# One key tile between a head's scores and its exponential, GpSimd in program order, one slot for reciprocals and result, and filler matmuls moved to later attention units

## The chip, the cores and the metric

The kernel runs on one core of a Trainium2 chip. The time is device microseconds of one execution of the program. The time before is the median of three runs. One more execution was recorded by the hardware profiler; all rows shown here come from that one.

## The reference

An encoder layer is run over two requests that share their weights: a sample of 1024 tokens and a prompt of 256, each with 16 learned meta tokens in front (1040 and 272 positions, width 1024, float32 throughout). The part that matters here is the attention and what follows it at once:

```python
def attention_block(qb, k, v):
    scale = HEAD_DIM ** -0.5
    s = jnp.einsum('bqhgd,bshd->bhgqs', qb, k).astype(jnp.float32) * scale
    p = jax.nn.softmax(s, axis=-1).astype(v.dtype)
    return jnp.einsum('bhgqs,bshd->bqhgd', p, v)
...
    g_attn = jax.nn.sigmoid(z[..., o3:o4])
    g_four = jax.nn.sigmoid(z[..., o4:])
...
    a = bidirectional_gqa(q, k, v) @ w_attn_o
    fo = fourier_mix(f) @ w_four_o
    merged = g_attn * a + g_four * fo
    x = x + merged @ w_out
```

There are 8 query heads of width 64 in 2 groups; each group of 4 shares one key head and one value head. Before this stage come the norm, the input projections and a Fourier branch; after it the merge, the output projection and a SwiGLU network.

## The kernel before

**Precision.** Every product is made of float32 operands split into a high and a low part (`split`), three matmuls for one (`three`, lines 231 to 233).

**Attention.** `attention` goes over units: a query tile of 128 tokens and a key group, four heads each. The prompt's tiles 8 and 9 come first (4 units), then the sample's tiles 0 to 7 (16 units). For one head (lines 994 to 1024):

- PE computes the scores of all keys into a PSUM tile `S` (line 1001): two matmuls for the prompt's 272 keys, six for the sample's 1040. `S` has one buffer. A sample head takes it whole, so the next head's scores wait for this head's exponential; three prompt heads fit in it side by side.
- VectorE takes the negated maximum (line 1006).
- ScalarE takes the exponential into a slot `p`, with the row's sum behind it (line 1013); VectorE later replaces the sum by its reciprocal (line 1019).

**The second half of a unit** is an object `Second`. It has one turn for each key tile: 9 in a sample unit, 3 in a prompt unit. A turn transposes a key tile of the four heads' probabilities on PE (line 915, two PSUM buffers `pt`), copies the high part on ScalarE (line 926) and subtracts for the low part on VectorE (line 927). The product with the values (lines 948, 949, 953, PSUM `pv`) follows some turns later. The last turn takes the 16 meta keys and the column of reciprocals, whose transposed row VectorE copies to a slot `rc` (line 919); SP writes it to DRAM and reads it back broadcast over 64 partitions (line 956). The two halves of `pv` are copied to a slot `ao` by ScalarE and VectorE (957, 958), added and multiplied by the reciprocals on GpSimd (959, 960), and stored to `a_d` (964).

The turns of a unit begin one head after its last head. `turns(0)` runs them between the next unit's maximum and exponential, `turns(1)` behind the exponential. The count for each call spreads what is left evenly over eight half heads: a sample unit gets 2 in front and 1 behind in its first head, then 1 and 1 three times.

**Filler.** After each half, `attention` yields a kind, and `gates` (a `Filler` around `gate_gen`) runs matmuls of the gate projection (tile `g`) until the debt `FILL[kind]` is paid: 12 units of weights by 768 columns, 576 matmuls in all, in steps of three. A step of 512 columns counts 640, one of 256 columns 320. If no unit is waiting for its second half, 1000 is added. What is left runs after the last key tile, beside the loads of the merge.

**Order.** In this stage PE, ScalarE and VectorE run in program order (`manual_schedule`). GpSimd and SP get their order from the framework's scheduler. On GpSimd there are also the low parts of the filler's weights (line 585) and, from the 97th yield on, one step per head of `fourier_parts`: memsets, casts (line 1069) and subtractions for the Fourier tail.

**Slots.** All tiles in SBUF come from 27 single slots and 7 triples. A slot that is given back goes to the end of a queue; whoever gets it next waits until its last reader is done.

**After attention** `load_af` reads `a_d` back (line 1100) and splits it (215, 216); `merge` multiplies the Fourier part (tile `fo`) and then the attention part (tile `m`), the sample's second half of tokens last.

Of the kernel before, what the change touches and what calls it, by code (L numbers as in the profile page):

```python
# [12 lines left out]
ALU = mybir.AluOpType  # L13
# [4 lines left out]
P = 128  # L18
# [4 lines left out]
HD = 64  # L23
# [28 lines left out]
LEAD = (2, 2, 2, 2, 2, 3, 3)  # L52
FINISH = (1, 3, 5, 7, 9)
LAG = 6000
XLOAD = 3
DVELO = (1,)
THIRDS = ((512, 1024), (0, 256), (256, 512))
# [79 lines left out]
def f32(ap):  # L137
    return ap.bitcast(F32)
# [44 lines left out]
class Kernel:  # L183
# [377 lines left out]

    FILL = {"s": 420, "p": 500, "end": 480, "drain": 900}

    def gate_gen(self, chunks, lo_engine):

# [312 lines left out]
    def attention(self, ps, tiles, tag_s, tag_v):  # L880


        nc, sl = self.nc, self.sl
        units = [(t, g) for t in tiles for g in range(NKV)]
        q = self.q

        def load_q(i):
            if i < len(tiles):
                self.load_q(tiles[i])

        load_q(1)

        mt = sl.get("mt", F32R)
        nc.gpsimd.memset(f32(mt[:, :1024]), 0.0)

        class Second:


            def __init__(me, i, t, g, ps4, slots):
                me.i, me.t, me.g, me.ps4, me.slots = i, t, g, ps4, slots  # L900
                n = 8 if t < 8 else 2
                me.keys = [(self.V[i if t < 8 else 8 + i], P, i * P) for i in range(n)]
                me.keys.append((self.V[10], N_META, n * P))
                me.j, me.pv = 0, None

            def left(me):
                return len(me.keys) - me.j

            def turn(me):
                V, rows, col = me.keys[me.j]  # L910
                pt = ps.tile([P, 512], F32, tag="tr", name=f"pt{me.t}{me.g}{me.j}")
                last = me.left() == 1
                for h in range(4):
                    m = rows + last
                    nc.tensor.transpose(pt[:m, h * P : (h + 1) * P], me.ps4[h][:, col : col + m], self.ident[:])  # L915
                if last:

                    me.rc = sl.get("rc")
                    nc.vector.tensor_copy(me.rc[:m, 512:1024], pt[:m, :])
                    nc.sync.dma_start(self.rc_d[me.t][me.g : me.g + 1, :], me.rc[rows:m, 512:1024])  # L920
                    pT, b = None, me.i % 2 * 512
                    hi, lo = mt[:rows, b : b + 512], mt[32 : 32 + rows, b : b + 512]
                else:
                    pT = sl.get("pT", F32R)
                    hi, lo = pT[:, :512], pT[:, 512:1024]
                nc.scalar.copy(hi, pt[:rows, :])  # L926
                nc.vector.tensor_tensor(lo, pt[:rows, :], f32(hi), op=ALU.subtract)  # L927

                if len(late) >= 2 and not (late[0][1] == 0 and len(late) == 2):
                    product()  # L930
                    if len(late) == 2:
                        product()
                late.append((me, me.j, pT))
                me.j += 1
                if me.j == len(me.keys):
                    sl.put(*me.slots)

        late = deque()

        def product():  # L940
            me, j, pT = late.popleft()
            t, g = me.t, me.g
            if j == 0:
                me.pv = ps.tile([P, 512], F32, tag=tag_v, name=f"pv{t}{g}")
            V = me.keys[j][0]
            vst = V[:, g * P : (g + 1) * P]
            if pT is not None:
                nc.tensor.matmul(me.pv[:], vst, pT[:, :512], start=j == 0, stop=False)
                nc.tensor.matmul(me.pv[:], vst, pT[:, 512:1024], start=False, stop=False)
                sl.put(pT)  # L950
                return
            b = me.i % 2 * 512
            nc.tensor.matmul(me.pv[:], vst, mt[:, b : b + 512], start=False, stop=True)
            aos = sl.get("ao")

            nc.sync.dma_start(me.rc[:HD, :512], self.rc_d[t][g].partition_broadcast(HD))
            nc.scalar.copy(aos[:HD, :512], me.pv[HD:P, :])
            nc.vector.tensor_copy(aos[:HD, 512:1024], me.pv[:HD, :])
            nc.gpsimd.tensor_tensor(aos[:HD, :512], aos[:HD, :512], aos[:HD, 512:1024], op=ALU.add)
            nc.gpsimd.tensor_tensor(aos[:HD, :512], aos[:HD, :512], me.rc[:HD, :512], op=ALU.mult)  # L960
            sl.put(me.rc)
            off = (t % 4) * P if t < 8 else (t - 8) * P
            dst = self.a_d[t // 4][:].rearrange("(h d) n -> d h n", d=HD)
            nc.sync.dma_start(
                dst[:, 4 * g : 4 * g + 4, off : off + P], aos[:HD, :512].rearrange("d (h n) -> d h n", h=4)
            )
            sl.put(aos)

        queue, n, divide, S = deque(), 0, None, None

        def turns(k):

            for me, ready in list(queue):
                if n < ready:
                    return
                for _ in range(-(-me.left() // (2 * (ready + 4 - n) - k))):
                    me.turn()
                if me.left():
                    return
                queue.popleft()  # L980

        for i, (t, g) in enumerate(units):
            if g == 0:
                i0 = tiles.index(t)
                load_q(i0 + (2 if i0 < 3 else 1))
            if t < 8:
                seq, L, cuts = "s", LS, (0, 264, 776, LS)
            else:
                seq, L, cuts = "p", LP, (0, LP)

            per, wide = SLOT // (L + 1), L + 1
            ps4, slots = [], []
            for h in range(4):
                hq = q[t][:, (4 * g + h) * P : (4 * g + h + 1) * P]

                if S is None or t < 8:
                    S = ps.tile([P, 1536], F32, tag=tag_s, name=f"S{t}{g}{h}")
                base = 248 if t < 8 else (4 * i + h) % 3 * 512
                for lo, hi in zip(cuts, cuts[1:]):
                    for v in range(2):  # L1000
                        nc.tensor.matmul(  # L1001
                            S[:, base + lo : base + hi], hq, self.kT[seq][g][v][:, lo:hi], start=v == 0, stop=v == 1
                        )
                sm = self.small.tile([P, 4], F32, tag="sm", name="sm", bufs=4)
                nb = sm[:, 0:1]
                nc.vector.tensor_reduce(nb, S[:, base : base + L], axis=AX.X, op=ALU.max, negate=True)  # L1006
                turns(0)
                if divide:
                    divide()
                if h % per == 0:  # L1010
                    slots.append(sl.get("p"))
                p = slots[-1][:, (h % per) * wide : (h % per + 1) * wide]
                self.last_exp = nc.scalar.activation(  # L1013
                    p[:, :L], S[:, base : base + L], AF.Exp, bias=nb, accum_out=p[:, L:wide]
                )
                yield "end" if i + 1 == len(units) else seq, 0, False

                def divide(x=p[:, L:wide]):
                    nc.vector.reciprocal(x, x)

                ps4.append(p)
                turns(1)
                yield "end" if i + 1 == len(units) else seq, 0 if queue else 1000, True
                n += 1
            if g == NKV - 1:
                sl.put(q.pop(t))
                if t == 9:
                    sl.put(*self.kv_slots[4:6])
                if t == tiles[-1]:
                    sl.put(*self.kv_slots[:4])  # L1030
            queue.append((Second(i, t, g, ps4, slots), n + 1))
        divide()
        while queue:
            for half in range(2):
                turns(half)
                yield "drain", 0, True
            n += 1
        while late:
            product()
        sl.put(mt, *self.kv_slots[6:])  # L1040


# [231 lines left out]
    def w_out(self, tiles, ps, then=None, apart=False):  # L1274
# [37 lines left out]
        for half in range(2):  # L1312
# [15 lines left out]
            for kk in range(4):  # L1328
                i = half * 4 + kk
                need(i + 1)  # L1330
                if apart and kk >= 2:
                    need(i + 3)
                if i == XLOAD:
                    for t in tiles:
# [43 lines left out]
    def second_norm(self, u, v, chunk, off, gf, ps):  # L1378
# [3 lines left out]
        hs = [self.h2.pop(t) for t in (u, v)]  # L1382
        yield LAG

# [366 lines left out]
    def build(self):  # L1751
        sl = self.sl
# [23 lines left out]
        units = self.ffn_units()  # L1776
        w1 = self.w_out((4, 6, 5, 7), ps_e, units, True)
        w02 = self.w_out((0, 2, 1, 3, 8, 9), ps_e, w1)
        m = self.merge(w02)
        with self.psum("pd", {"S": (1, 1536), "tr": 2, "pv": 1, "g": 2}) as ps:  # L1780
            E = mybir.EngineType
            self.mm = ps, "g"
            with self.tc.manual_schedule(engines={E.PE, E.Activation, E.DVE}):
                later = self.later = deque()
                parts = self.fourier_parts()
                for i, (kind, more, slack) in enumerate(self.attention(ps, [8, 9] + list(range(8)), "S", "pv")):
# [179 lines left out]
```

## Time and profile before

| | us |
|---|---|
| median of three runs | 1725.2 (1723.81 to 1730.75) |
| the profiled execution | 1728.47 |
| its span, first to last instruction | 1726.7 |
| attention, first scores to the last exponential | 317 to 644 |
| PE busy in the span | 1648.2 (95%) |

Times in the rows are microseconds from the span's start unless a row says ns. In a row of the timeline stand start, duration, engine, line, operation, out<-in, shape and count, and in brackets the idle time of the engine before it with what ended it. In a group's row (line, engine, operation, shape, count) stand the busy time in us and the mean ns of one, then the idle time before them by releaser. A matmul's duration runs to its modelled end, while the next one starts earlier. Names like `hT0l` or `fx` in place of `pT` or `wgl` are slots that were part of a triple.

### The profile page before, as it was taken

How to read it: one execution, taken by the hardware profiler on the slowest of the kernel's cores; microseconds unless marked ns; L12 is line 12 of the kernel's file. 1: busy time of each engine (PE TensorE's matmuls, PEld its weight loads, DVE VectorE, ACT ScalarE, POOL GpSimd, SP SyncE). 2: the span in 40 equal slices, each digit the busy share in tenths (PEclk: the TensorE clock that was granted, in tenths of full speed). 3: DMA queues.
4: the chain of work that ended last, by engine and by line, in shares of the span. 5: the costliest groups of instructions: out<-in, count | busy, mean ns of one | idle time of the engine just before them, and what ended most of it. 6: DMA issues, size and time to landing. Idle time of an engine off the chain costs nothing.

```text
span 1726.7 us, 26025 instructions
## 1 busy us (share of the span) xinstructions
PE 1648.2 (95%) x9739; PEld 1474.7 (85%) x9739; DVE 1100.5 (64%) x2028; ACT 727.4 (42%) x1463; POOL 355.1 (21%) x400
## 2 busy tenths in 40 slices
PE   7999999989979998999989999999999999999998
PEld 6888879867767786878879999999999998888886
DVE  5563555346756766661489676667666768765685
ACT  6433333446656765551355222222232224444444
POOL 3451443232242323563352000000000000000002
PEclk9999999999999999999999999999999999999999
DMA  6135231421111226533432222322232237653534
GB/s 247 42 124 176 98 115 46 149 62 62 50 49 59 65 80 222 164 128 117 176 142 81 89 72 86 103 90 88 91 103 91 69 122 258 207 179 93 164 96 153
DMA packets 92454, 198.76 MB, mean 115 GB/s; under 512 B 10230, under 2 KB 41622, under 8 KB 92328
## 3 DMA queue, kind: packets, MB, share of 16 engines
q1 hardware_dynamic: 82296, 179.63, 31.4%
q10 hardware_dynamic: 8400, 12.53, 2.1%
q0 software_dynamic: 1632, 4.93, 0.9%
q8 instruction: 77, 1.26, 0.3%
q14 instruction: 49, 0.40, 0.1%
HBM read 141.58 MB, written 55.47 MB: 114 GB/s over the span
## 4 chain that ended last, share of the span: by engine, by line
PE 72%; DVE 9%; ACT 7%; issue 4%; POOL 4%; DMA 3%; SPq 0%; ACTq 0%; POOLq 0%; DVEq 0%
PE i L233 10%; PE i L231 10%; PE i L232 10%; PE o L233 5%; PE o L232 5%; PE o L231 5%; PE S L1001 4%; ACT p L1013 2%; PE pt L915 2%; PE g L231 2%; PE g L232 2%; PE g L233 2%; DVE sm L1006 2%; PE wo L232 2%; PE wo L233 2%
## 5 line engine op out<-in xcount | busy, mean ns | idle before, releaser
L1458 ACT CAST w<-wi 128x512 fp32r<-128x512 f32 x168 | 104.0, 621 | 272.1 <-PE i L233 219.0
L231 PE MATMUL i<-A,w 128*128 128x384 f32 x616 | 209.1, 339 | 3.0 <-ACT w L1458 2.7
L233 PE MATMUL i<-A,w 128*128 128x384 f32 x616 | 209.0, 340 | 2.3 <-POOL w L1460 2.3
L232 PE MATMUL i<-A,w 128*128 128x384 f32 x616 | 208.6, 339 | 0.0
L231 PE MATMUL i<-Ah,w 128*128 128x256 f32 x616 | 173.0, 281 | 0.7 <-DVE sc L1514 0.7
L232 PE MATMUL i<-Al,w 128*128 128x256 f32 x616 | 173.0, 281 | 0.0
L233 PE MATMUL i<-Ah,w 128*128 128x256 f32 x616 | 173.0, 281 | 0.0
L240 POOL TENSOR_SCALAR fin0r<-fin0ss 128x1 f32<-128x1 f32 x1 | 0.8, 785 | 755.7 <-ACT X L248 755.7
L1460 DVE TENSOR_TENSOR w<-wi,w 128x512 fp32r<-128x512 f32 x154 | 105.4, 686 | 28.8 <-ACT w L1458 28.3
L927 DVE TENSOR_TENSOR pT<-pt,pT 128x512 fp32r<-128x512 f32 x117 | 80.0, 686 | 65.5 <-ACT pT L926 65.0
L231 PEld LDWEIGHTS i<-A,w 128*128 128x128 f32 x616 | 116.7, 189 | 3.6 <-ACT w L1458 2.9
L233 PEld LDWEIGHTS i<-A,w 128*128 128x128 f32 x616 | 116.7, 189 | 3.0 <-POOL w L1460 2.9
L231 PEld LDWEIGHTS i<-Ah,w 128*128 128x128 f32 x616 | 116.1, 188 | 1.4 <-DVE sc L1514 0.9
L232 PEld LDWEIGHTS i<-A,w 128*128 128x128 f32 x616 | 116.7, 189 | 0.0
L233 PEld LDWEIGHTS i<-Ah,w 128*128 128x128 f32 x616 | 116.2, 189 | 0.0
L232 PEld LDWEIGHTS i<-Al,w 128*128 128x128 f32 x616 | 116.1, 189 | 0.0
L1006 DVE TENSOR_REDUCE sm<-S 128x1 f32<-128x1040 f32 (+1 forms) x80 | 86.4, 1081 | 36.8 <-PE S L1001 32.2
L926 ACT CAST pT<-pt 128x512 fp32r<-128x512 f32 x117 | 68.4, 585 | 76.6 <-PE pt L915 65.1
L915 PE MATMUL pt<-ident,p 128*128 128x128 f32 (+1 forms) x624 | 94.7, 275 | 3.4 <-DVE pT L927 2.7
L1013 ACT ACTIVATE p<-S,sm 128x1040 f32<-128x1040 f32 (+1 forms) x80 | 80.1, 1001 | 37.2 <-DVE sm L1006 28.5
L915 PEld LDWEIGHTS pt<-ident,p 128*128 128x128 f32 (+1 forms) x624 | 72.4, 135 | 16.3 <-DVE pT L927 6.0
L233 PE MATMUL o<-wfo,act 128*128 128x512 f32 (+1 forms) x212 | 82.0, 388 | 1.6 <-DVE act L1592 1.6
(812 smaller groups left out, 4529.9 us busy)
## 6 DMA issues: line engine op xcount, KB each, us to landing
wi<-w_fi SPq DMA_DIRECT2D x48, 512.0 KB
act_d<-sc SPq DMA_DIRECT2D x77, 192.0 KB
wg<-w_g SPq DMA_DIRECT2D x24, 512.0 KB
act<-act_d SPq DMA_DIRECT2D x37, 320.0 KB
wfo<-w_fo SPq DMA_DIRECT2D x21, 512.0 KB
X<-act_d SPq DMA_DIRECT2D x31, 320.0 KB
act_d<-sc SPq DMA_DIRECT2D x77, 128.0 KB
gt<-gate SPq DMA_DIRECT2D x32, 256.0 KB
```

Of the source, the lines that this page charges most:

```text
L231: mm(out, sh, mh, start=first and i == 0, stop=False)
L232: mm(out, sh, ml, start=False, stop=False)
L233: mm(out, slo, mh, start=False, stop=last and i == n - 1)
L240: nc.gpsimd.tensor_scalar(r[:p, 0, :n], ss, scale, eps, op0=ALU.mult, op1=ALU.add)
L915: nc.tensor.transpose(pt[:m, h * P : (h + 1) * P], me.ps4[h][:, col : col + m], self.ident[:])
L926: nc.scalar.copy(hi, pt[:rows, :])
L927: nc.vector.tensor_tensor(lo, pt[:rows, :], f32(hi), op=ALU.subtract)
L1001: nc.tensor.matmul(S[:, base + lo : base + hi], hq, self.kT[seq][g][v][:, lo:hi], start=v == 0, stop=v == 1)
L1006: nc.vector.tensor_reduce(nb, S[:, base : base + L], axis=AX.X, op=ALU.max, negate=True)
L1013: self.last_exp = nc.scalar.activation(p[:, :L], S[:, base : base + L], AF.Exp, bias=nb, accum_out=p[:, L:wide])
L1458: nc.scalar.copy(w[:, :512], src)
L1460: eng.tensor_tensor(w[:, 512:1024], src, f32(w[:, :512]), op=ALU.subtract)
```

## The change

1. `turns`: the count is now a goal for each head, a quarter of the key tiles per head, and at most one turn stands between maximum and exponential. A sample unit has (1 in front, 2 behind), then (1, 1) three times; a prompt unit has one in front in each of three heads.
2. The slot `rc` is gone: the row of reciprocals is copied into partitions 64 to 80 of `ao`, which is taken at the last turn instead of at the last product, and the broadcast goes into the half of `ao` that the addition has read. So it follows the addition.
3. The multiplication, the store and the giving back of `ao` are kept in `leaving` and issued at the third call of `leaves` after the product, two heads later; in the drain `leaves` is called after each half.
4. GpSimd is added to the engines that run in program order.
5. `FILL` has new values, the first sample unit has its own kind `first`, the addition without a waiting unit is 150 instead of 1000, and the drain's kind is `end` while two units wait.

```diff
+FIRST = 4
-    FILL = {"s": 420, "p": 500, "end": 480, "drain": 900}
+    FILL = {"s": 550, "p": 150, "first": 1150, "end": 550, "drain": 600}
...
-                    me.rc = sl.get("rc")
-                    nc.vector.tensor_copy(me.rc[:m, 512:1024], pt[:m, :])
-                    nc.sync.dma_start(self.rc_d[me.t][me.g : me.g + 1, :], me.rc[rows:m, 512:1024])
+                    ao = me.ao = sl.get("ao")
+                    nc.vector.tensor_copy(ao[64 : 64 + m, :512], pt[:m, :])
+                    nc.sync.dma_start(self.rc_d[me.t][me.g : me.g + 1, :], ao[64 + rows : 64 + m, :512])
...
-            aos = sl.get("ao")
-            nc.sync.dma_start(me.rc[:HD, :512], self.rc_d[t][g].partition_broadcast(HD))
-            nc.scalar.copy(aos[:HD, :512], me.pv[HD:P, :])
-            nc.vector.tensor_copy(aos[:HD, 512:1024], me.pv[:HD, :])
-            nc.gpsimd.tensor_tensor(aos[:HD, :512], aos[:HD, :512], aos[:HD, 512:1024], op=ALU.add)
-            nc.gpsimd.tensor_tensor(aos[:HD, :512], aos[:HD, :512], me.rc[:HD, :512], op=ALU.mult)
-            sl.put(me.rc)
...
+            ao = me.ao
+            nc.scalar.copy(ao[:HD, :512], me.pv[HD:P, :])
+            nc.vector.tensor_copy(ao[:HD, 512:1024], me.pv[:HD, :])
+            nc.gpsimd.tensor_tensor(ao[:HD, :512], ao[:HD, :512], ao[:HD, 512:1024], op=ALU.add)
+            nc.sync.dma_start(ao[:HD, 512:1024], self.rc_d[t][g].partition_broadcast(HD))
+            def leave():
+                nc.gpsimd.tensor_tensor(ao[:HD, :512], ao[:HD, :512], ao[:HD, 512:1024], op=ALU.mult)
...
+                sl.put(ao)
+            leaving.append([2, leave])
+        def leaves(all=False):
+            while leaving and (all or leaving[0][0] <= 0):
+                leaving.popleft()[1]()
+            for x in leaving:
+                x[0] -= 1
...
-                for _ in range(-(-me.left() // (2 * (ready + 4 - n) - k))):
+                goal = -(-len(me.keys) * min(n - ready + 1, 4) // 4)
+                if k == 0:
+                    goal = min(goal, me.j + 1)
+                while me.j < goal:
                     me.turn()
...
-                yield "end" if i + 1 == len(units) else seq, 0, False
+                kind = "end" if i + 1 == len(units) else "first" if t < 8 and i <= FIRST else seq
+                yield kind, 0, False
...
                 turns(1)
-                yield "end" if i + 1 == len(units) else seq, 0 if queue else 1000, True
+                leaves()
+                yield kind, 0 if queue else 150, True
...
                 turns(half)
-                yield "drain", 0, True
+                leaves()
+                yield "drain" if len(queue) < 2 else "end", 0, True
...
         while late:
             product()
+        leaves(True)
...
-            with self.tc.manual_schedule(engines={E.PE, E.Activation, E.DVE}):
+            with self.tc.manual_schedule(engines={E.PE, E.Activation, E.DVE, E.Pool}):
```

More of the change, by code (lines that the diff above doesn't have):

```diff
@@ L936, in turn @@
                     sl.put(*me.slots)
-        late = deque()
+        late, leaving = deque(), deque()
         def product():
@@ L953, in product @@
             nc.tensor.matmul(me.pv[:], vst, mt[:, b : b + 512], start=False, stop=True)
-            aos = sl.get("ao")
[L956 to L960, printed above, removed]
-            sl.put(me.rc)
[L962 to L967, printed above, removed]
+            ao = me.ao
[5 more added lines that the diff above has]
+                nc.gpsimd.tensor_tensor(ao[:HD, :512], ao[:HD, :512], ao[:HD, 512:1024], op=ALU.mult)
+                off = (t % 4) * P if t < 8 else (t - 8) * P
+                dst = self.a_d[t // 4][:].rearrange("(h d) n -> d h n", d=HD)
+                nc.sync.dma_start(
+                    dst[:, 4 * g : 4 * g + 4, off : off + P], ao[:HD, :512].rearrange("d (h n) -> d h n", h=4)
+                )
+                sl.put(ao)
[5 more added lines that the diff above has]
+                x[0] -= 1
         queue, n, divide, S = deque(), 0, None, None
```

## The prediction

> **What bounds the kernel now.** The page first, then stretches, waits and timeline.
>
> ```profile
> PE 1648.2 (95%) x9739; PEld 1474.7 (85%) x9739; DVE 1100.5 (64%) x2028; ACT 727.4 (42%) x1463; POOL 355.1 (21%) x400
> ```
>
> TensorE (PE) is busy for 95% of the span, an average that hides the stage in question: every instruction that the diff touches lies between 317 and 690 us. So I read the table of stretches there, cut where the program turns from prompt attention to the first sample unit, the other 15 sample units, the drain and the tail. Columns: length, busy time of PE, weight loads, VectorE (DVE), ScalarE (ACT), GpSimd (POOL), granted clock, DMA share, GB/s.
>
> ```profile
> 317.10:359.50 42.40, 40.66 (x240) 34.22 (x238) 17.28 (x45) 21.07 (x57) 12.80 (x10) 1.00 0.32 106
> 359.50:377.80 18.30, 14.17 (x78) 11.63 (x77) 8.55 (x13) 8.57 (x15) 5.11 (x4) 0.91 0.25 73
> 377.80:643.80 266.00, 243.06 (x1457) 202.78 (x1458) 181.36 (x281) 170.70 (x303) 73.69 (x62) 0.99 0.18 56
> 643.80:667.40 23.60, 20.64 (x132) 17.61 (x130) 12.07 (x20) 12.21 (x22) 2.58 (x2) 1.00 0.73 249
> 667.40:690.00 22.60, 17.77 (x91) 15.48 (x92) 15.72 (x24) 11.52 (x20) 11.77 (x16) 0.85 0.62 207
> ```
>
> The prompt stage is full; the other four leave PE idle for 4.1, 22.9, 3.0 and 4.8 us. The same stretches for the filler alone (tile g, the gate product) show why: the full stage has most of it.
>
> ```profile
> 317.10:359.50 42.40, 31.79 (x161) 1.00 0.32 106
> 359.50:377.80 18.30, 7.28 (x37) 0.91 0.25 73
> 377.80:643.80 266.00, 71.45 (x312) 0.99 0.18 56
> ```
>
> 161 of the filler's 576 matmuls run where attention needs PE for little, and the long sample stage, which waits, has 312 for 60 heads. Who waits there, from the table of waits (total, times, longest):
>
> ```profile
> PE S L1001 <- ACT p L1013: 20.0, 20, 7.2
> ACT pT L926 <- DMA a_d<-ao: 4.8, 5, 1.3
> ```
>
> Scores of the next head wait for the exponential of this one, because a sample head has the one S buffer. The timeline shows two shapes of it. The starts of five heads, and the copies in front of the third one's exponential:
>
> ```profile
> 519.93 0.28 PE L1001 MATMUL S<-hT0l,qT 128*128 128x264 f32 x1
> 523.68 1.22 PE L1001 MATMUL S<-kT,qT 128*128 128x264 f32 x6
> 527.60 1.12 PE L1001 MATMUL S<-kT,qT 128*128 128x264 f32 x6
> 530.10 0.59 ACT L926 CAST pT<-pt 128x512 fp32r<-128x512 f32 x1 [0.32 <-PE pt L915]
> 530.71 0.58 ACT L957 COPY p<-pv 64x512 f32<-64x512 f32 x1
> 531.32 1.13 ACT L1013 ACTIVATE p<-S,sm 128x1040 f32<-128x1040 f32 x1
> 532.59 1.22 PE L1001 MATMUL S<-kT,qT 128*128 128x264 f32 x6 [0.31 <-ACT p L1013]
> 536.63 1.10 PE L1001 MATMUL S<-kT,qT 128*128 128x264 f32 x6
> ```
>
> They start 3.75, 3.92, 4.99 and 4.04 us apart. The long one is the head with three key tiles: two come before the exponential, and the second one's copy plus the copy of the finished result (0.59 + 0.58) hold ScalarE. That is 1.1 us once in four heads. The other shape comes once:
>
> ```profile
> 508.22 3.21 POOL L1069 CAST hT0l<-x64r 8x1024 fp32r<-8x1024 f32 x3
> 511.51 1.25 POOL L960 TENSOR_TENSOR ao<-ao,rc 64x512 f32<-64x512 f32 x1
> 512.79 1.13 ACT L1013 ACTIVATE p<-S,sm 128x1040 f32<-128x1040 f32 x1 [6.63 <-POOL ao L960]
> 514.06 0.59 PE L1001 MATMUL S<-hT0l,qT 128*128 128x264 f32 x1 [7.20 <-ACT p L1013]
> ```
>
> Three casts that GpSimd was given ahead of the division kept the result's slot, the exponential wanted that slot, and PE stood 7.2 us. Its matmuls then run at half clock (0.59 for a shape that took 0.28), for a window:
>
> ```profile
> 514.80:518.30 3.50, 3.50 (x13) 3.00 (x12) 2.29 (x3) 1.51 (x3) 0.38 (x1) 0.53 0.36 97
> ```
>
> **The change part by part.** No matmul is added or removed, so the sum is over idle time.
>
> *Filler.* The debts, counted by the code's own costs (a step of three matmuls is 640 at 512 columns, 320 at 256; a filler unit is 7680, all twelve 92160): prompt stage 32 yields x 500 + 10 x 1000 = 26.0 us, now 32 x 150 + 7 x 150 = 5.85; first sample unit 8 x 420 + 2 x 1000 = 5.36, now 8 x 1150 + 150 = 9.35; the other 15 units 112 x 420 + 8 x 480 = 50.9, now 112 x 550 + 8 x 550 = 66.0; drain 9.0, now 550 + 9 x 600 = 5.95; the rest, run after the last key tile, 0.92, now 5.01. On the chip the unit is larger:
>
> ```profile
> 317.42 0.40 PE L231 MATMUL g<-hT1h,wgh 128*128 128x512 f32 x1
> 319.98 0.40 PE L233 MATMUL g<-hT1h,wgl 128*128 128x512 f32 x1
> ```
>
> First and last of twelve in a row: 2.56 / 11 = 0.233 us from start to start, so 0.70 for 640: factor 1.09.
>
> *Prompt stage.* PE loses 20.15 x 1.09 = 22.0 us of work. If PE stayed the bound, 40.66 - 22.0 = 18.7 us would be left. But then the other engines' turns show, from the groups of this stage:
>
> ```profile
> L1013 ACT ACTIVATE p<-S,sm 128x272 f32<-128x272 f32 x16 | 7.8, 487 | 11.5 <-DVE sm L1006 10.2 <-issue 1.3
> L1006 DVE TENSOR_REDUCE sm<-S 128x1 f32<-128x272 f32 x16 | 7.0, 439 | 17.7 <-PE S L1001 17.0 <-ACT wgh L584 0.5 <-issue 0.2
> L927 DVE TENSOR_TENSOR pT<-pt,pT 128x512 fp32r<-128x512 f32 x5 | 3.5, 692 | 4.7 <-ACT pT L926 4.7
> L926 ACT CAST mt<-pt 16x512 fp32r<-16x512 f32 x3 | 1.7, 578 | 4.7 <-DVE rc L919 4.7
> L958 DVE COPY ao<-pv 64x512 f32<-64x512 f32 x2 | 1.4, 683 | 0.0
> ```
>
> A head with a key tile costs VectorE 0.44 + 0.69 and a reciprocal, ScalarE 0.49 + 0.58 and a read of the sum, in turn: about 1.5 us with the hand-overs; one without, 1.0. A unit of three and one, with the result's two copies and the last tile's copy ahead of ScalarE's, is about 6.5; the first, without tiles, 4.0. 4.0 + 3 x 6.5 = 23.5. PE is then busy for 18.7 of 23.5, and the clock may fall:
>
> ```profile
> 361.35:364.76 3.41, 1.56 (x11) 1.48 (x11) 0.92 (x3) 1.73 (x3) 1.10 (x2) 0.96 0.58 183
> 371.60:375.00 3.40, 1.97 (x15) 1.67 (x14) 1.47 (x4) 2.16 (x4) 1.45 (x2) 1.00 0.13 30
> ```
>
> After the first (1.56 of 3.41 busy) the clock was halved, after the second (1.97 of 3.40) not. The first four prompt heads come near that, so I add one half-clock window, 3.4/2 = 1.7 us. I take 25.2: a gain of 17.2, with 18.7 below and, above, 42.4 (nothing gained if latency alone sets the head).
> The Trainium skill, "TensorE: Matmul & The Clock Gate", Part 1, has the clock fall only after a whole idle window of some 3.4 us; no such pause is to be expected here, and by that rule the stage would be 23.5 and the sum 1.7 lower. The trace disagrees: the longest wait in the first sample unit, where the clock fell, was 1.9 us.
>
> ```profile
> PE S L1001 <- ACT p L1013: 3.3, 2, 1.9
> ```
>
>
> *First sample unit.* Work other than filler 14.17 - 7.28 = 6.9, filler 9.35 x 1.09 = 10.2: 17.1 against 18.30, a gain of 1.2. The extra filler fills the waits and the half clock (0.91) that the unit has now.
>
> *One key tile in front, the others behind.* Each unit's double now runs behind the exponential, and so does the copy of the result. What is late next: those copies and subtractions keep VectorE, and the following head's maximum starts up to 0.9 us later (a subtraction of 0.69 and the result's copy of 0.68 more, less some 0.5 by which PE brings its scores later). It is covered while PE has over 3.75 + 0.9 = 4.6 us of work in that head, which the larger filler gives in most. With it, PE's work in the 60 heads: 243.06, less 20 waits x 0.16 (a matmul's modelled end, 0.39, against its 0.23 spacing) = 3.2, less 3.5 x 0.47 = 1.7 of slow clock, plus 15.1 x 1.09 = 16.5: 254.7. I add 4.0, an estimate, for heads that get only one filler step and fall back on the chain (3.75 above) and for late maxima: 258.7 against 266.0, a gain of 7.3. Ends: 11.3 with no idle; a loss of 5 if the long head stays (15 x 0.8 = 12 more).
>
> *GpSimd in program order; division two heads later.* The casts then come one per head and the division stands at its place, so the 7.2 us stall and its clock go (inside the 7.3). What queues behind the division on GpSimd is the next filler weights' subtraction, off the path. On SP the broadcast now waits for GpSimd's sum instead of the reciprocals' landing; weight and q loads behind it have a filler unit's time or two units to spare: nothing.
>
> *Reciprocals in the result's slot.* No instruction changes its shape. The broadcast starts after the sum; for the last unit that is on the path:
>
> ```profile
> 667.47 0.50 PE L953 MATMUL pv<-mt,v 128*128 128x512 f32 x1 [2.06 <-DVE mt L927]
> 668.09 0.46 SPq L956 DMA_DIRECT2D p<-rc_d  x1
> 669.39 1.37 POOL L959 TENSOR_TENSOR ao<-ao 64x512 f32<-64x512 f32 x1 [12.70 <-DVE ao L958]
> 672.20 1.35 POOL L960 TENSOR_TENSOR ao<-ao,p 64x512 f32<-64x512 f32 x1 [1.44 <-DMA p<-rc_d]
> 688.42 0.50 PE L232 MATMUL m<-fx,hT0l 128*128 128x512 f32 x1 [1.33 <-DVE fx L216]
> ```
>
> Broadcast to division took 4.1 us; issued at 669.39 + 1.37 = 670.8 instead of 668.1 it makes the chain to the merge 21.0 + 2.7 = 23.7. The drain is 3.05 x 1.09 = 3.3 shorter, and the 4.5 of filler now behind the last product lies in the longer chain. Tail and drain: -3.3 + 2.7 = -0.6 (-4 to +4, as the loads there, DMA share 0.73, move).
>
> **Sum.** 17.2 + 1.2 + 7.3 + 0.6 = 26.3 us. The profiled execution took 1728.5 (span 1726.7); the median of the runs is 3.3 lower, 1725.2, so 1702.2 by its own time is 1698.9 by the median. No change can be told within 0.5%, 8.6 us.
>
> **The rivals.**
> 1. *The prompt stage stays long*: 36 us instead of 25.2, since VectorE and ScalarE wait for each other at every tile (4.7 us in each of two groups above). 1709.7. For it: idle of 17.7 before the maxima. Against: most of that is PE busy with filler. 0.17.
> 2. *The long head only moves*: two tiles behind delay the next maximum as much as two in front did; 12 us come back, 1710.9. Against: the next head has PE work to cover it. 0.12.
> 3. *GpSimd's order was not the cause*: the stall stays, 7.2 + 1 of clock, 1707. Against: the three casts stand right in front. 0.07.
> 4. *Slower*: the slot, now held two heads longer out of the same 27, is reused before its result has landed, and ScalarE waits in each of 16 sample units. It decides from 26.3 / 16 = 1.6 us a unit; at 2.5 a unit it is 1739. For it: 4.8 us of such waits now. Against: the longest is 1.3, and the slot is given back 8 us later while its landing moves by 2.7. 0.06.
>
> **How the numbers follow.** The forecast has 0.55, nearly all of it between 1688 (prompt stage 21, sample stage without idle, tail -3) and 1706 (tail +4, prompt stage 28). Rivals 1 to 3 have 0.36, of which 0.29 lies below 1716.6, where 0.5% begins, and 0.07 above it, where each is larger than priced. Rival 4 has 0.06, mishaps together 0.03. So faster 0.84, within 0.5% 0.08, slower 0.08; and 1688 to 1717 holds 0.80.
>
> **What would show it.** The prompt heads at 1.0 to 1.7 us instead of 2.6; the wait of S for p from 20 us to about 4; no wait of an exponential for GpSimd; long heads at 4.3 to 4.7; PE's filler matmuls about 36 in the prompt stage and 410 in the 15 units. Wrong it would be with a prompt stage over 33 us, PE at half clock there for several windows, or copies that wait for a_d in every unit.

## The result and the profile after

The changed kernel takes 1712.4 us (median of five runs, 1710.69 to 1718.76) against 1726.7 for the kernel before in the same comparison: ratio 0.9921, 95% interval 0.9896 to 0.9945. It is faster by 14.3 us where the prediction said 26.3. The profiled execution took 1710.69 us, span 1708.8.

The stretches of the changed kernel, cut at the same places as those of before (prompt stage, first sample unit, the other 15, drain, tail; columns as there):

```profile
316.80:355.70 38.90, 25.84 (x113) 18.78 (x111) 17.45 (x44) 17.02 (x47) 6.36 (x5) 0.82 0.20 67
355.70:373.80 18.10, 17.26 (x105) 14.69 (x105) 8.85 (x15) 8.54 (x16) 6.29 (x5) 1.00 0.18 57
373.80:628.00 254.20, 250.96 (x1552) 217.32 (x1553) 180.45 (x281) 173.23 (x312) 78.76 (x67) 1.00 0.22 66
628.00:651.00 23.00, 22.40 (x142) 19.13 (x140) 13.26 (x23) 12.52 (x23) 5.50 (x3) 1.00 0.84 269
651.00:674.00 23.00, 16.26 (x85) 14.64 (x84) 12.65 (x21) 11.31 (x20) 10.37 (x15) 0.85 0.64 207
```

The prompt stage went from 42.4 to 38.9, the first sample unit from 18.3 to 18.1, the other 15 from 266.0 to 254.2, and what follows (span less the end of that stretch) from 1082.9 to 1080.8. With 0.3 at the start that is 3.5 + 0.2 + 11.8 + 2.1 + 0.3 = 17.9, the difference of the two spans. The filler (tile `g`) did move:

```profile
316.80:355.70 38.90, 9.42 (x35) 0.82 0.20 67
355.70:373.80 18.10, 10.90 (x63) 1.00 0.18 57
373.80:628.00 254.20, 91.07 (x405) 1.00 0.22 66
```

35 and 405 matmuls, where 36 and 410 were expected. So the prompt stage lost 126 filler matmuls and only 3.5 us. The waits between scores, maximum and exponential, prompt stage first, then the sample stage with the one wait for a slot (the names are those of slots, so an exponential's `p` is called `ao` in some rows):

```profile
DVE sm L1021 <- PE S L1016: 14.5, 14, 1.6
PE S L1016 <- ACT p L1028: 11.8, 12, 1.9
```
```profile
PE S L1016 <- ACT p L1028: 1.7, 2, 1.2
PE S L1016 <- ACT ao L1028: 1.1, 1, 1.1
ACT ao L1028 <- DMA a_d<-ao: 1.7, 1, 1.7
```

In the sample stage the wait of S for the exponential fell from 20.0 to 2.8 us (1.7 + 1.1), and ScalarE waits once for a slot that a result is still leaving. The second head of a sample unit, the long one, has a median of 4.4 us (5.1 before). In the prompt stage PE waits 11.8 us for p, and the maximum 14.5 us for scores. The same wait of PE in the prompt stage of the kernel before, which the prediction did not weigh:

```profile
PE S L1001 <- ACT p L1013: 1.7, 6, 0.5
```

Filler stood between there: with the filler put back into the changed kernel (e4 below) this wait is 2.9 us. The changed kernel's timeline:

```profile
318.71 0.52 PE L1016 MATMUL S<-kTp,qT 128*128 128x272 f32 x2 [0.72 <-ACT p L1028]
319.34 0.44 DVE L1021 TENSOR_REDUCE sm<-S 128x1 f32<-128x272 f32 x1 [1.55 <-PE S L1016]
319.81 0.49 ACT L1028 ACTIVATE p<-S,sm 128x272 f32<-128x272 f32 x1 [1.16 <-DVE sm L1021]
320.45 0.52 PE L1016 MATMUL S<-kTp,qT 128*128 128x272 f32 x2 [0.51 <-ACT p L1028]
322.18 0.52 PE L1016 MATMUL S<-kTp,qT 128*128 128x272 f32 x2 [0.51 <-ACT p L1028]
```

Scores, maximum, exponential, and only then the next head's scores: 1.73 us from head to head, though three prompt heads lie side by side in `S` and the next head writes other columns. The prediction had taken them to overlap and a head without a key tile to last 1.0. From scores to scores, the first prompt unit takes 7.0 us and the other three 10.5, 10.7 and 10.5, where 4.0 and three times 6.5 were counted. Two signs that the prediction had named for being wrong are there: a prompt stage over 33 us, and PE at half clock in several windows of it (four, the last section shows three).

### The profile page after: what moved, and what is told of

It reads as the page before. It is cut to its first block, busy times and chain, and to the rows that moved or that the text cites. A ratio compares the mean times of both kernels' runs of the same rounds, so it can differ in the third digit from the quotient of the medians.

```text
span 1708.8 us, 25999 instructions
## 1 busy us (share of the span) xinstructions
PE 1645.1 (96%) x9739; PEld 1479.5 (87%) x9739; DVE 1096.7 (64%) x2028; ACT 725.4 (42%) x1463; POOL 355.8 (21%) x400
## 4 chain that ended last, share of the span: by engine, by line
PE 75%; DVE 9%; ACT 5%; issue 4%; POOL 3%; DMA 3%; SPq 0%; ACTq 0%; POOLq 0%; DVEq 0%
PE i L234 10%; PE i L232 10%; PE i L233 10%; PE o L234 5%; PE o L233 5%; PE o L232 5%; PE S L1016 4%; PE pt L916 3%; PE g L234 2%; PE g L232 2%; PE g L233 2%; PE pv L949 2%; PE pv L950 1%; PE wo L233 1%; PE wo L234 1%
## 5 line engine op out<-in xcount | busy, mean ns | idle before, releaser
L928 DVE TENSOR_TENSOR pT<-pt,pT 128x512 fp32r<-128x512 f32 x110 | 75.5, 687 | 51.0 <-ACT pT L927 50.9
L916 PE MATMUL pt<-ident,p 128*128 128x128 f32 (+1 forms) x507 | 90.7, 279 | 0.5 <-DVE hT0l L928 0.4
L927 ACT CAST pT<-pt 128x512 fp32r<-128x512 f32 x110 | 64.1, 583 | 49.7 <-PE pt L916 47.1
L234 PE MATMUL o<-wfo,act 128*128 128x512 f32 (+1 forms) x212 | 82.2, 388 | 2.0 <-DVE act L1611 2.0
L233 PE MATMUL o<-wfo,act 128*128 128x512 f32 (+1 forms) x212 | 81.8, 386 | 0.0
L232 PE MATMUL o<-wfo,act 128*128 128x512 f32 (+1 forms) x212 | 81.6, 388 | 0.0
```

The costliest lines, as they stand in the source:

```text
L232: mm(out, sh, mh, start=first and i == 0, stop=False)
L233: mm(out, sh, ml, start=False, stop=False)
L234: mm(out, slo, mh, start=False, stop=last and i == n - 1)
```

## The experiments

All twelve at a glance, each timed in five rounds. The three stages are read from the stretches of each profile, cut as above (the sample stage from the second unit's first scores to 3.7 us behind the last head's first scores). Ratios are to the kernel before as timed beside each (its medians there: 1726.6 to 1727.3).

| kernel | prompt | first unit | sample | median us | ratio (95%) |
|---|---|---|---|---|---|
| before | 42.4 | 18.3 | 266.0 | 1726.6 | |
| changed | 38.9 | 18.1 | 254.2 | 1712.4 | 0.9921 (0.9896 to 0.9945) |
| e1, changed + three S tiles | 23.4 | 20.1 | 254.6 | 1699.6 | 0.9842 (0.9829 to 0.9854) |
| e8, e1 + filler spread | 27.8 | 19.4 | 252.6 | 1702.2 | 0.9863 (0.9849 to 0.9878) |
| e10, before + three S tiles | 39.3 | 16.7 | 265.5 | 1723.9 | 0.9984 (0.9972 to 0.9997) |
| e4, changed, filler in the prompt | 40.2 | 16.8 | 252.7 | 1714.3 | 0.9925 (0.9913 to 0.9937) |
| e5, before + filler moved | 40.6 | 21.0 | 273.7 | 1732.9 | 1.0037 (1.0025 to 1.0049) |
| e2, changed, GpSimd by the scheduler | 38.8 | 18.1 | 255.7 | 1714.6 | 0.9924 (0.9910 to 0.9937) |
| e6, before + GpSimd in order | 42.3 | 16.7 | 262.3 | 1724.6 | 0.9990 (0.9981 to 0.9998) |
| e3, changed, old turns | 41.3 | 21.7 | 265.5 | 1732.1 | 1.0026 (1.0014 to 1.0038) |
| e7, before + new turns | 41.0 | 16.7 | 269.7 | 1726.6 | 1.0004 (0.9995 to 1.0012) |
| e9, before + turns + slot and delay | 40.2 | 16.8 | 251.3 | 1711.6 | 0.9909 (0.9890 to 0.9928) |
| e11, changed, slot rc and no delay | 36.5 | 18.0 | 268.1 | 1721.1 | 0.9969 (0.9955 to 0.9982) |
| e12, changed, no delay | 38.9 | 18.1 | 322.7 | 1782.9 | 1.0333 (1.0309 to 1.0357) |

**The prompt stage: one tile or three (e1, e10, e8).** Two theories: A, the single tile makes the heads take turns; B, VectorE and ScalarE wait for each other at every key tile, whatever the tiles of `S` are.

e1 gives each prompt head a tile of its own and goes back to the wide tile for the sample:

```diff
...
-                if S is None or t < 8:
-                    S = ps.tile([P, 1536], F32, tag=tag_s, name=f"S{t}{g}{h}")
-                base = 248 if t < 8 else (4 * i + h) % 3 * 512
+                if t < 8 and not wide_S:
+                    pool.__exit__(None, None, None)
+                    pool = self.psum("pS", {tag_s: (1, 1536)})
+                    pool.__enter__()
+                    wide_S = True
+                S = pool.tile([P, 1536 if wide_S else 512], F32, tag=tag_s, name=f"S{t}{g}{h}")
+                base = 248 if t < 8 else 0
...
```

> The changed kernel, with each prompt head's scores in a PSUM tile of their own (three tiles of 512 columns that rotate) instead of thirds of one tile. Theory A: the order of instructions treats S as one thing, so in the prompt stage too the next head's scores wait for this head's exponential, and the chain scores, maximum, exponential (1.73 us a head without a key tile) sets the stage. Then the stage falls from 38.9 us to 24 to 28, its waits of S for p (17.3 + 11.8 us) to under 5, and the ratio to before is 0.983 to 0.987. Theory B: VectorE and ScalarE waiting for each other at every key tile set it. Then the stage stays at 36 to 39 us and the ratio at 0.992.

Measured 1699.6 us. The first two stretches of its profile, and three heads of its timeline:

```profile
318.04:341.48 23.44, 17.71 (x113) 15.10 (x111) 16.13 (x44) 16.51 (x47) 6.38 (x5) 0.97 0.29 109
341.48:361.62 20.14, 19.44 (x105) 17.09 (x105) 8.83 (x15) 8.57 (x16) 6.31 (x5) 0.87 0.16 53
```
```profile
318.04 0.41 PE L1023 MATMUL S<-kTp,qT 128*128 128x272 f32 x2
318.97 0.42 PE L1023 MATMUL S<-kTp,qT 128*128 128x272 f32 x2
319.23 0.49 ACT L1035 ACTIVATE p<-S,sm 128x272 f32<-128x272 f32 x1 [0.40 <-DVE sm L1028]
319.92 0.41 PE L1023 MATMUL S<-kTp,qT 128*128 128x272 f32 x2
```

The second head's scores start before the first head's exponential, and the heads follow at 0.94 us instead of 1.73. The same 113 matmuls take 23.4 us instead of 38.9. PE's waits for p in the stage fell from 11.8 to one of 2.5 us, where the first sample head takes the wide tile. A holds: the program's order treats the tile as one object. The stage is even a little under the expected 24 to 28. The first unit gives back 2.0 of it (granted clock 0.87). e1 is 12.8 us faster than the changed kernel.

e10 puts the same three tiles into the kernel before.

> The kernel before with a tile of S for each of three prompt heads, nothing else. Theory: before, the prompt stage is set by PE (40.7 of 42.4 us busy, 26 us by its own costs of it filler), so the hand-over through the one tile costs little: 1.7 us of waits of S for p there. Prompt stage 40 to 42, ratio 0.998 to 1.000; so the three tiles and the moved filler gain only together. Rival, the one tile cost time before too: prompt stage under 38, ratio 0.997 or less.

Measured: prompt stage 39.3, a little under the expected 40, the whole 2.7 us faster. With 26 us of filler in the stage PE is the bound, and the tiles have little to give:

```profile
317.65:356.90 39.25, 39.08 (x238) 34.42 (x237) 16.95 (x45) 20.93 (x56) 12.83 (x10) 1.00 0.36 113
```

The tiles gain 12.8 us in the changed kernel and 2.7 in the kernel before. That the moved filler makes the difference fits PE's 39.1 busy of 39.3 us here, but the changed kernel with three tiles and the old filler was not run.

e8 takes e1 and puts some filler back into the prompt stage, whose PE idles 5.7 us (beside the edit of e1):

```diff
-    FILL = {"s": 550, "p": 150, "first": 1150, "end": 550, "drain": 600}
+    FILL = {"s": 510, "p": 300, "first": 1000, "end": 510, "drain": 600}
-                yield kind, 0 if queue else 150, True
+                yield kind, 0 if queue else 300, True
```

> The changed kernel with a tile of S for each of three prompt heads, as in e1_three_S, and a little filler put back: in the prompt stage 300 for a half head and 300 more without a waiting unit (12 us by its own costs instead of 5.9), 510 instead of 550 in the sample units, 1000 instead of 1150 in the first one. Theory: the prompt stage has idle PE time left (17.8 us busy of 23.5), so 6 us more there cost it 2 to 4, and the first sample unit and the others give back 5 to 6; 1694 to 1698, ratio 0.981 to 0.983. Rival: the heads of the prompt are set by PE in part already and the sample units lose nothing with less filler, as when 18.6 us were put back with one tile; then the time is that of e1_three_S or more, ratio 0.984 to 0.987.

The rival was right. The stage grew by 4.4, the first unit and the others gave back 0.7 and 2.0: 1702.2 us, no better than e1. Of all kernels run here, e1 has the lowest median, but its interval and that of e8 overlap.

**The filler (e4, e5).** e4 is the changed kernel with 420 for sample halves and the first unit, 500 in the prompt, 480 at the end and 1000 without a waiting unit; the drain's value stays.

```diff
-    FILL = {"s": 550, "p": 150, "first": 1150, "end": 550, "drain": 600}
+    FILL = {"s": 420, "p": 500, "first": 420, "end": 480, "drain": 600}
-                yield kind, 0 if queue else 150, True
+                yield kind, 0 if queue else 1000, True
```

> The changed kernel with the filler of before in the prompt and sample units (p 500 and 1000 without a waiting unit, first 420, s 420, end 480); drain as changed. Theory A: the filler taken from the prompt stage had covered a chain that did not get shorter. Put back, the prompt stage is 41 to 43 us (38.9 without it), and the 60 heads of the 15 sample units, relieved of 15 us of filler, take 238 to 243 us instead of 254: ratio 0.983 to 0.987. Rival C: the sample heads need that filler, since their own chain holds them at the pace they have; they stay at 250 or more, and the ratio is 0.994 or above.

Neither theory's time came: the total is that of the changed kernel (ratio 0.9925). The prompt stage took 40.2 us with four times the filler (26 us by the code's costs against 5.85). The sample stage took 252.7 with less of it: 250 or more, as C had it, and far from A's 238 to 243. With one tile, filler is nearly free in the prompt stage, and taking it out of the sample stage gains 1.5 us. e5 gives the kernel before the new filler values and nothing else:

```diff
-    FILL = {"s": 420, "p": 500, "end": 480, "drain": 900}
+    FILL = {"s": 550, "p": 150, "first": 1150, "end": 550, "drain": 600}
...
-                yield "end" if i + 1 == len(units) else seq, 0 if queue else 1000, True
+                yield kind, 0 if queue else 150, True
...
```

> The kernel before with the filler's new values alone (prompt stage 5.9 us of filler by its own costs instead of 26, the sample units more); old turns, slot rc, GpSimd by the scheduler, S as one tile. Theory: with one tile for S the prompt heads take turns whatever the filler is (38.9 us in the changed kernel, 40.2 with 26 us of filler put back), and a sample head with old turns is set by the chain of scores, maximum, copies, exponential, not by PE's filler. So the prompt stage is 38 to 41 us, the sample heads stay near 262, and the wait of S for p in the sample units stays above 10 us. Ratio 0.997 to 1.005. Rival, filler is the gain: it then keeps most of the 14 us, ratio 0.990 to 0.994.

1.0037. The prompt stage is as expected, the sample stage not unchanged but 7.7 us longer; its stretch and its wait for slots:

```profile
379.00:652.73 273.73, 256.60 (x1553) 218.17 (x1552) 181.67 (x281) 174.43 (x311) 77.88 (x65) 0.99 0.21 62
```
```profile
ACT pT L926 <- DMA a_d<-ao: 9.5, 7, 2.9
```

PE's busy time there is 13.5 more (256.60 against 243.06), its idle time only 5.8 less, and ScalarE waits 9.5 instead of 4.8 us for slots that a result is still leaving. Moving the filler is no gain by itself; it is a small loss.

**GpSimd in program order (e2, e6).** e2 takes `E.Pool` out of `manual_schedule` again.

> The changed kernel with GpSimd ordered by the scheduler again. Theory: casts go ahead of a division once more and one exponential waits 5 to 8 us for its slot, ratio 0.995 to 0.997. Rival: the division is issued two heads later and its slot is given back after that, so nothing waits, ratio 0.992.

0.9924, as the rival had it: no stall in the sample stage, and the order adds nothing to the rest. The wait of S for p there (1.3 more, once, where the slot is called `ao`):

```profile
PE S L1016 <- ACT p L1028: 2.5, 3, 1.2
```

e6 adds `E.Pool` to the kernel before and nothing else.

> The kernel before with GpSimd in program order and nothing else. Theory: the three casts no longer stand ahead of the division, so the stall of 7.2 us and its half clock go and the sample stage is 7 to 9 us shorter; ratio 0.995 to 0.996. Rival: in program order GpSimd stands at the division until the broadcast has landed, and the casts behind it come late, so that another wait takes the place; ratio 0.998 or more. Second rival: the stall is gone only because the division is given two heads; then it is still in this kernel and the ratio is 1.000.

0.9990: the theory's gain did not come, and the time is that of the first rival. The stall has shrunk, not gone. Around 508 us, where 7.2 us stood:

```profile
506.04 1.25 POOL L959 TENSOR_TENSOR ao<-ao 64x512 f32<-64x512 f32 x1 [4.01 <-DVE p L1019]
507.37 1.25 POOL L960 TENSOR_TENSOR ao<-ao,rc 64x512 f32<-64x512 f32 x1
508.66 1.13 ACT L1013 ACTIVATE p<-S,sm 128x1040 f32<-128x1040 f32 x1 [3.42 <-POOL ao L960]
509.93 0.39 PE L1001 MATMUL S<-hT0l,qT 128*128 128x264 f32 x1 [3.98 <-ACT p L1013]
```

The casts are gone from in front of the division, which follows the sum at once, and PE still stands 3.98 us: the exponential is given the slot whose division is just running. So the reason is not the first rival's late casts. The casts were about half of the stall; the early return of the slot is the rest.

**The turns, the slot and the delay (e3, e7, e9, e11, e12).** e3 puts the old count of turns back into the changed kernel.

```diff
-                goal = -(-len(me.keys) * min(n - ready + 1, 4) // 4)
-                if k == 0:
-                    goal = min(goal, me.j + 1)
-                while me.j < goal:
+                for _ in range(-(-me.left() // (2 * (ready + 4 - n) - k))):
```

> The changed kernel with the old count of turns (two key tiles in front of the exponential in each unit's first head). Theory: the long head comes back, 4.9 to 5.0 us in each of 15 units where it has 4.0 to 4.5 now; waits of S for p in the sample stage go from 2.8 to 10 us or more, and the ratio is 0.995 to 0.998. Rival: the larger filler alone covers that head, the waits stay under 5 us and the ratio at 0.992.

1.0026, where 0.995 to 0.998 was expected: without the new turns the whole gain is lost, not a part of it. The sample stage is 265.5, the long head is back (median 5.0 us), and the prompt stage and the first unit are 2.4 and 3.6 longer too. So the turns are needed. But they are not enough, as e7 shows, the new turns alone in the kernel before (with 450 for 420).

> The kernel before with the new turns alone, and 450 instead of 420 for a half of a sample head (3.4 us of filler more in the sample units, taken from the end, since the slots run out otherwise). Theory: the long heads go from 5.0 to 4.3 us and the waits of S for p in the sample units to under 10 us, most of them the one stall of 7.2 us if that stays; the sample heads come to 249 to 255 us, the prompt stage stays at 41 to 43. Ratio 0.992 to 0.995. Rival, the turns gain only where more filler covers the later maxima: sample heads 258 or more, ratio 0.998 or more.

1.0004, sample stage 269.7, the time of the rival. (The profiled execution took 1731.2 us, and its attention starts 5.2 us later than in the kernel before; the stages leave that out.) Two of ScalarE's waits there, the second for a division not yet made:

```profile
ACT pT L926 <- DMA a_d<-ao: 13.0, 7, 2.2
ACT p L1016 <- POOL ao L960: 7.7, 3, 2.9
```

With the kernel before, these two were 4.8 and 6.6. What the turns free, waits for slots take. So a new theory against the rival's (more filler is needed): the turns gain only with the later return of the slot. e9 tests it: turns, slot and delay, with the filler of e4 and GpSimd left to the scheduler.

> The changed kernel without its filler values (as in e4_prompt_filler: 420 for a half of a sample head, 500 in the prompt, 1000 without a waiting unit) and without GpSimd's program order: so of the change only the new turns, the reciprocals in the result's slot and the division two heads later. Theory (the turns gain only with the later return of the slot, since with the turns alone ScalarE waited 28 us in the sample units for slots whose result was not stored yet, and the long heads' gain was eaten): these two parts are the whole gain, sample heads 249 to 252 us, prompt stage about 40, ratio 0.991 to 0.994. Rival, the filler is what makes the turns gain: sample heads 256 or more, ratio 0.996 or more.

```profile
375.06:626.33 251.27, 241.09 (x1467) 202.94 (x1468) 180.40 (x281) 168.92 (x303) 72.53 (x62) 1.00 0.20 58
```

0.9909: turns and slot with delay are the whole gain of the change, without the moved filler and without GpSimd's order. e11 keeps the turns, filler and order, and takes slot and delay back:

```diff
-                    ao = me.ao = sl.get("ao")
-                    nc.vector.tensor_copy(ao[64 : 64 + m, :512], pt[:m, :])
+                    me.rc = sl.get("rc")
+                    nc.vector.tensor_copy(me.rc[:m, 512:1024], pt[:m, :])
...
-            leaving.append([2, leave])
+            leave()
```

> The changed kernel with its turns, filler and GpSimd in program order, but with a slot of its own for the reciprocals and the division, the store and the return of the slots right behind the product, as before. Theory: the waits of ScalarE for a slot whose result is not stored come back (28 us in all with the turns alone, one of 1.7 us in the changed kernel), sample heads 258 to 266 us, ratio 0.997 to 1.003. Rival, the turns with more filler do it without the slot: sample heads 250 to 254, ratio 0.991 to 0.994.

```profile
ACT pT L927 <- DMA a_d<-ao: 11.0, 7, 2.0
ACT p L1028 <- POOL ao L962: 7.3, 5, 1.9
```

The waits are back and the sample stage is 268.1, 2.1 above the theory's range and far from the rival's; the ratio, 0.9969, is at the range's lower edge, because the prompt stage and the tail came out shorter. e12 keeps the reciprocals in the result's slot and takes away the delay alone:

```diff
-            leaving.append([2, leave])
+            leave()
```

> The changed kernel with the division, the store and the return of the slot issued right behind the product instead of two heads later; the reciprocals stay in the result's slot. Theory A (what counts is when the slot goes back to the end of the queue): it goes back two heads too early, is handed out before its result has landed, ScalarE waits in many of the 16 units, and with the broadcast now behind the sum by 2.7 us more than with a slot of its own; sample heads 258 to 270, ratio 0.997 to 1.005. Theory B (what counts is the number of slots, one more free without rc): sample heads 250 to 254, ratio 0.991 to 0.994.

1782.9 us, 70.5 more than the changed kernel: of theory A's kind, far beyond its size (sample stage 322.7, where 258 to 270 was expected). One unit of it:

```profile
384.33 1.27 POOL L959 TENSOR_TENSOR ao<-ao 64x512 f32<-64x512 f32 x1 [8.24 <-DVE ao L958]
385.63 0.47 SPq L960 DMA_DIRECT2D ao<-rc_d  x1
388.94 1.28 POOL L963 TENSOR_TENSOR ao<-ao 64x512 f32<-64x512 f32 x1 [3.33 <-DMA ao<-rc_d]
390.25 0.61 SPq L966 DMA_DIRECT2D a_d<-ao  x1
392.88 0.58 ACT L927 CAST pT<-pt 128x512 fp32r<-128x512 f32 x1 [5.60 <-DMA a_d<-ao]
```

From the start of the sum to the copy that was given the slot it takes 8.6 us: the broadcast, now behind the sum, the division, the store. ScalarE stands 5.6 of them. The granted clock is 0.92 over the stage. Shown so: sharing the slot without the delay is a heavy loss, and the two together are needed beside the turns. Not tried is the delay with a slot `rc` of its own, so their shares are not separated further.

## Why the prediction was right and wrong

- **Prompt stage, the step that failed:** 42.4 to 25.2 was forecast, 38.9 came; 13.7 us too little. By the profiled executions 8.4 us of gain are missing in all (26.3 against 17.9), so this step outweighs the others, which together gave more than forecast. The step priced the stage by VectorE's and ScalarE's turns, 4.0 + 3 x 6.5, as if heads side by side in `S` overlapped. They do not: scores, maximum and exponential of one head follow each other through the one tile, at 1.73 us a head without a key tile where 1.0 was counted, and the units take 7.0 and three times 10.5 to 10.7. PE idled 38.90 - 25.84 = 13.1 us where 4.8 were counted, and was busy 5.4 longer than the 18.7 + 1.7 of the sum, much of it at a lower clock (0.82 over the stage).
- **Where the warning stood:** not in the idle of 17.7 before the maxima. Putting that down to filler was right: with three tiles and the old filler (e10) the maximum still waits 15.0 us for scores. It stood in PE's six short waits for p (1.7 us), which with three tiles (e10) are gone.
- **What was right in the step:** once the tiles are apart (e1), the stage takes 23.4 us with PE busy for 17.7, against 23.5 without the slow clock and 18.7 forecast, and a head without a key tile takes 0.94. So the total fits once the premise is met. That each part was sized right is not shown: from scores to scores e1's units take 3.1, 3.7, 6.9 and 9.8, because scores now run ahead. (A slip: without the half-clock window of 1.7 the sum of gains would be 1.7 higher, not lower; it is the time that would be lower.)
- **First sample unit:** 1.2 forecast, 0.2 measured. PE was busy for 17.3, the work counted was 17.1; the unit has 0.84 of idle that the sum left out.
- **The other 15 units:** 7.3 forecast, 11.8 measured. The idle time was right (3.2 against 4.0); PE's work was put 3.7 too high, 254.7 against 250.96. That the long heads go is right (e3 has them back). That the extra filler covers the late maxima was not needed: with the old filler the stage is 251.3 (e9). That the gain needs the delayed return was not seen: the prediction put the slot and GpSimd's order at nothing beyond the 7.2 us stall.
- **GpSimd's order:** named as what takes the stall away. e2 has no stall without it, and e6 has 3.98 of it left with it. The rival "GpSimd's order was not the cause" was half right: the order alone (e6) takes away about half of the stall; e2 and e9 have none without it, but with the later return of the slot that the exponential waited for.
- **Tail and drain:** -0.6 forecast, -2.1 measured; what agreement there is, is luck, since the parts are off by more. Up to the last product it is 5.6 us shorter (3.3 forecast). From there to the product of the merge that the prediction showed (at 688.42 before) it takes 27.3 us, where 23.7 were forecast and 21.0 had been. What follows is 2.9 shorter, which the sum did not count. In the middle part PE has a new wait of 6.1 us for ScalarE's copy of the Fourier part. That copy comes behind ScalarE's split of the attention output, which waits 5.7 us until the last result's store has landed: so the later broadcast reaches PE by ScalarE's order too, which the prediction did not count:

```profile
646.06 0.50 PE L954 MATMUL pv<-mt,v 128*128 128x512 f32 x1 [0.47 <-DVE mt L928]
658.56 1.04 ACT L216 CAST afh<-af 128x1024 fp32r<-128x1024 f32 x1 [5.69 <-DMA a_d<-ao]
662.65 0.64 PE L1190 MATMUL fo<-hT0l,y 72*128 72x328 f32 x1 [6.11 <-ACT fst L1203]
673.38 0.39 PE L233 MATMUL m<-y,hT0l 128*128 128x512 f32 x1
```

- **The rivals:** the first, a prompt stage of 36 us, came nearest in that stage (38.9), but for another reason: it named VectorE and ScalarE waiting for each other at every key tile, and the heads without a key tile are serial too. The second, that the long head only moves, gave 1710.9, nearest to 1712.4 in time by luck; it is refuted, since the stage's waits of S for the exponential fell to 2.8 us. The fourth, a slot reused before its result has landed, is not in the changed kernel, but it is the mechanism that e7, e11 and e12 show; priced at 2.5 us a unit, it costs 70.5 / 16 = 4.4 with the shared slot and no delay.

## What to carry to other kernels

Where a program's order is kept by tiles, columns of one tile are no ring of buffers: give each turn a tile, and look for a wait of a writer for the last reader in the profile, even a short one under filler. Before work is moved out of a stage that looks full, ask what sets its length once the work is gone, and read it from the hand-overs instead of the busy times. A slot that goes back to a queue costs nothing only if its last reader is done when it is handed out again: keep the return as late as the slowest reader, before anything shortens the loop around it.

## What was not expected of the hardware

The clock fell with TensorE far from idle. Stretches of 3.4 us of the changed kernel's prompt stage, cut where its granted clock (third column from the end) changes:

```profile
319.34:322.76 3.42, 2.34 (x10) 1.19 (x8) 1.02 (x4) 1.66 (x5) 0.05 (x1) 1.00 0.42 165
322.76:326.17 3.41, 1.74 (x9) 1.26 (x10) 1.02 (x4) 1.16 (x4) 1.21 (x1) 1.00 0.00 0
326.17:329.58 3.41, 2.26 (x11) 1.85 (x10) 1.64 (x4) 1.06 (x3) 0.00 (x0) 0.50 0.00 0
329.58:333.00 3.42, 2.97 (x10) 1.60 (x9) 1.61 (x4) 1.07 (x3) 0.00 (x0) 0.50 0.00 0
333.00:336.41 3.41, 1.45 (x6) 0.97 (x7) 1.63 (x5) 2.13 (x6) 1.27 (x1) 1.00 0.00 1
336.41:339.82 3.41, 3.41 (x13) 2.98 (x13) 1.20 (x3) 1.07 (x3) 0.00 (x0) 0.50 0.00 0
```

PE's longest wait for p in the stage was 1.9 us, none of these stretches is idle, and yet PE ran at half clock after those with 1.74 and 1.45 us busy, and not after the one with 2.34. The Trainium skill, "TensorE: Matmul & The Clock Gate", Part 1, has in its table of the two states the slow one set in after a whole idle window of about 3.4 us. These rows disagree with that: a window about half busy was not enough here, while e1's prompt stage, at 17.7 of 23.4 busy, kept 0.97. The runs give no exact share: later in the same trace, at 752.8 us, a stretch with 1.67 of 3.40 us busy was followed by one at full clock.
